# Sums of weight quarters in a feed-forward layer: from VectorE to accumulating transfers

## The chip, the cores and the metric

The kernel runs on one core of one Trainium2 chip, as one launch. The metric is the device time of that launch in microseconds (us); the kernel before takes 2193.0 us (median of 3 runs, 2192.62 to 2193.12). The profile names the engines so: PE is the matmul engine (TensorE) and PEld its weight loads, DVE is VectorE, ACT is ScalarE, POOL is GpSimd, SP the engine that issues the loads from memory. Every engine works through its own queue in order; semaphores tie the queues together. About 0.2% of the time (4.4 us) is what a measurement of this kernel tells from no change.

## The reference

One decoder block on 512 tokens of width 2048, in float32: RMS norm, one combined input projection, eight heads of dilated sliding-window attention and eight heads of sparse attention (compressed, selected and window branches mixed by gates), group norms, an output projection, and then the part that this case is about:

```python
hn2 = rmsnorm(h, norm2_g[l])
h = h + (jax.nn.silu(hn2 @ w_gate[l]) * (hn2 @ w_up[l])) @ w_down[l]
return rmsnorm(h, final_g)
```

`w_gate` and `w_up` are 2048 x 5632, `w_down` is 5632 x 2048.

## The kernel before, in words

**Three matmuls for one.** Each float32 operand is held as a high part (rounded to the matmul's format, `h`) and a low part (what is missing, `l`), and a product is three matmuls: high by high, high by low, low by high (L162 to 165 and L1002 to 1005).

**Weights.** Weights stream in on SP's queue. A unit is 128 x 1024 numbers, 512 KB; `load_to` (L102) puts it into one of four rotating buffers `raw` (`LA = 4`). A load may start when the buffer's last readers are done. Each unit is used as two *halves* of 512 columns; a half is a `Job` (L121). `Job.first` runs the job's `load` and `prep`, then rounds the half to `wh` on ACT (L134). `Job.second` makes `wl` on DVE (L137) and then runs the job's `post`. `wh` and `wl` have five rotating buffers each.

**The order of work.** The program is one order written out by hand. PE takes halves one after the other through `next_half` (L170): on its way it issues the `first` of the job three places ahead and the `second` of the one two places ahead, and runs what has been put off with `later(n, ...)`, that is, n halves after the present one. So within the queues of ACT and DVE the splits of coming weights stand between the evacuations of finished products.

**The feed-forward stage.** The 5632 columns of gate and up are worked in 44 blocks of 128 (`FB`, index f). In a block the weights form four quarters: gate0 (upper 1024 rows of the gate columns, called A11), up0 (A21), up1 (A22) and gate1 (A12), and the activations four quarters B11, B12, B21, B22 (row half by token half; 256 tokens each). Instead of eight products of quarters there are seven, P1 to P7, in the manner of Strassen and Winograd, each of 2 halves x 4 weight blocks x 3 matmuls of 256 columns:

| product | weights | activations |
|---|---|---|
| P1 | gate0 | B11 |
| P2 | gate1 | B21 |
| P3 | gate1 - (up0 + up1 - gate0) | B22 |
| P4 | up1 | T4 |
| P5 | up0 + up1 | T1 |
| P6 | up0 + up1 - gate0 | T2 |
| P7 | gate0 - up0 | T3 |

T1 to T4 are sums of activation quarters, made once by `terms` (L915). The sums of weight quarters are made anew in every block, in place in the `raw` buffers, by `comb` (L750) in `quad_jobs` (L743): four 128 x 512 operations on DVE per half column, eight per block. `ORDER0` is the order of the products in block 0, `ORDER` that in the others.

`product` (L990) issues the matmuls; P2 adds into P1's accumulator bank, and in blocks after the first P3 adds into P5's. `after` (L1020) reads the banks on ACT and DVE and puts gate and up together; `finish` (L1007) makes silu(gate) x up and splits it into high and low for the down product.

**Down products.** Every four blocks (`PH = 4`) the 16 row blocks of the down product for the last four column blocks are worked in (`down`, L1053). They stand between the products of blocks 4, 8, ..., 40: a *down job* is one load of 256 KB (`rawd`, two buffers), one split, and 12 matmuls of 512 columns. Blocks without them are called plain here: of blocks 1 to 43 these are 33, in 11 runs of three. The last down product comes after block 43 (`last`, L1091), with its weights (`fin`) in the `raw` buffers.

Of the kernel before, what the change touches and what calls it, by code (L numbers as in the profile page):

```python
# [71 lines left out]
def block_kernel(ctx: ExitStack, tc: tile.TileContext, xt, wst, wdn, smalls, wg, w2c, bias, ident_in, out):  # L72
# [24 lines left out]

    raws = {}
    state = {"dma": 0, "split": 0}
    LA = 4  # L100

    def load_to(n):  # L102
        while state["dma"] < min(n, len(units)):
# [66 lines left out]
    def next_half():  # L170
        i = pos["half"]
        pos["half"] += 1
        split_to(i + (AHEAD[i] if i < len(AHEAD) else 3 if i < len(jobs) - KB - 1 else 4))
        if i < n_plain:
            load_to(i // 2 + LA)
        while lag and lag[0][0] <= i:
            lag.popleft()[1]()
        j = jobs[i]
        return j.h, j.l
# [563 lines left out]
    def quad_jobs(f, order):  # L743

        u = base_u + 4 * f

        def q(i, k):
            return raws[u + i][:, 512 * k:512 * k + 512]

        def comb(o, a, b, op):  # L750
            return lambda: dve.tensor_tensor(o(), a(), b(), op=op)  # L751

        def nxt(i):
            return lambda: load_to(u + 4 + i + 1)

        r = {}
        for k in range(2):
            A11, A21, A22, A12 = (lambda i=i, k=k: q(i, k) for i in range(4))
            if f == 0:
                def s1(A11=A11, A21=A21, A22=A22):  # L760
                    comb(A11, A11, A21, OP.subtract)()
                    comb(A21, A21, A22, OP.add)()

                r["P1", k] = Job(A11, load=nxt(-1))
                r["P5", k] = Job(A21, prep=s1)
                r["P7", k] = Job(A11)
                r["P4", k] = Job(A22)
            else:
                r["P1", k] = Job(A11)
                r["P7", k] = Job(A11, prep=comb(A11, A11, A21, OP.subtract))  # L770
                r["P4", k] = Job(A22, post=comb(A21, A21, A22, OP.add))
                r["P5", k] = Job(A21)
            r["P6", k] = Job(A22, prep=comb(A22, A22, A11, OP.subtract))
            r["P2", k] = Job(A12)
            r["P3", k] = Job(A12, prep=comb(A12, A12, A22, OP.subtract))
        if f + 1 < FB:
            if f == 0:
                r["P6", 1].post = nxt(1)
                r["P3", 1].post = nxt(3)
            else:  # L780
                r["P6", 1].post = nxt(0)
                r["P5", 1].post = nxt(1)
                r["P3", 1].post = nxt(3)
        else:
            r["P6", 1].post = lambda: load_fin(1)
            r["P5", 1].post = lambda: load_fin(2)
            r["P3", 1].post = lambda: load_fin(LA)
        r["P1", 0].even = f in (1, 2) or f % 8 == 5
        return [r[p, k] for p in order for k in range(2)]

    ORDER0 = ("P1", "P5", "P2", "P7", "P4", "P6", "P3")
    ORDER = ("P1", "P7", "P4", "P6", "P5", "P2", "P3")

    def dn_job(p, nb):
        return Job(lambda: dn[p, nb], post=load_dn)
# [119 lines left out]
    def terms(nb):  # L915

        h, k, n = hs[:, nb, :], hs[:, nb % 8, :], nb % 8
        g, gk = gain2(nb), gain2(nb % 8)
        sq = ps.tile([128, S], F32, tag="sc", name="sq", bufs=2)
        t = ps.tile([128, S], F32, tag="t", name="tm", bufs=2)  # L920

        def stt(o, a, b, op):
            dve.scalar_tensor_tensor(o, a, b, t[:, LO] if op != OP.bypass else t[:, HI], op0=OP.mult, op1=op)

        def sums():
            if nb:
                dve.tensor_tensor(sacc, sacc, sq, op=OP.add)

        def squares():
            act.activation(sq if nb else sacc, h, AF.Square)  # L930

        if nb < 8:
            def s1():
                dve.tensor_tensor(t[:, LO], h[:, HI], h[:, LO], op=OP.subtract)
                squares()
                high("B11", n, h[:, LO], g)
                high("T1", n, t[:, LO], g)

# [12 lines left out]
        def s2():  # L951
            dve.scalar_tensor_tensor(t[:, LO], h[:, HI], g, t[:, LO], op0=OP.mult, op1=OP.subtract)
            sums()
            low("B21", n, h[:, LO], g)
            high("T3", n, t[:, LO])

        def s3():
            dve.scalar_tensor_tensor(t[:, HI], k[:, LO], gk, t[:, LO], op0=OP.mult, op1=OP.add)
            low("T3", n, t[:, LO])
            high("T2", n, t[:, HI])  # L960

        def s4():
# [24 lines left out]

    st = {}

    def product(f, name):  # L990
        key = {"P2": "P1", "P3": "P5" if f else "P3"}.get(name, name)
        if key == name:
            st[key] = banks[name]
        p = st[key][:, :256]
# [12 lines left out]
    def finish(f, g, u, c):  # L1007
# [3 lines left out]

        def up():
            dve.tensor_tensor(u, u, g, op=OP.mult)
            act.activation(h, u, AF.Copy)

        n = 0 if c == LO else 1
        later(n, up)
        later(n + 1, lambda: dve.tensor_tensor(l, u, h.bitcast(F32), op=OP.subtract))

    def after(f, name):  # L1020

# [3 lines left out]
        def add(o, a, b):  # L1025
            dve.tensor_tensor(o, a, b, op=OP.add)

        g, u = st.get("g"), st.get("u")
        if name == "P1":
            st["g"] = ft()  # L1030
            st["u"] = ft() if f else None
            act.activation(st["g"][:, LO], x("P1"), AF.Copy)
        elif name == "P6":
            add(g[:, HI], g[:, LO], x("P6"))
            add(u[:, LO], g[:, HI], x("P7"))
            if not f:
                dve.tensor_tensor(g[:, LO], x("P1"), st["r2"][:, LO], op=OP.mult)
                add(u[:, HI], u[:, LO], x("P5"))
                add(u[:, LO], u[:, LO], x("P4"))
                add(g[:, HI], g[:, HI], x("P5"))  # L1040
        elif name == "P5":
            add(u[:, HI], u[:, LO], x("P5"))
            add(u[:, LO], u[:, LO], x("P4"))
        elif name == "P2":
            dve.tensor_tensor(g[:, LO], x("P1"), st["r2"][:, LO], op=OP.mult)
            if f == FB - 1:
                finish(f, g, u, LO)
        elif name == "P3":
            add(g[:, HI], g[:, HI], x("P5" if f else "P3"))
            dve.tensor_tensor(g[:, HI], g[:, HI], st["r2"][:, HI], op=OP.mult)  # L1050
            finish(f, g, u, HI if f == FB - 1 else slice(0, 512))

# [18 lines left out]
    for kind, a, b in sched:  # L1071
# [5 lines left out]
        if f == 0:  # L1077
# [7 lines left out]
                st["u"] = ft()  # L1085
            if name in ("P1", "P6", "P3"):
                later(0 if name == "P1" else 1, lambda name=name: after(0, name))
        elif name in ("P1", "P6", "P5", "P2", "P3"):
# [145 lines left out]
```

## Time and profile before

| what | value |
|---|---|
| median of 3 runs | 2193.0 us |
| profiled execution | 2195.16 us |
| its span, first to last instruction | 2193.4 us |
| granted PE clock, mean | 0.996 |
| mean DMA rate, share of the 16 DMA engines taken by loads and stores | 105 GB/s, 33.2% |
| bytes read from and written to memory | 223.94 MB, 4.19 MB |
| loads of 512 KB into `raw` | 311 |
| loads of 256 KB into `rawd` | 160 |
| DVE sums in `raw` (L751) | 352, 241.7 us busy |

How to read the views: a group of instructions has its line, engine, operation, out<-in tiles with their shape and count, then busy time, mean ns of one, and the idle time of the engine just before them with what ended it. A wait has the waiting instruction, the one that released it, and total us, times, longest us. A row of a stage gives busy time and count of PE, PEld, DVE, ACT and POOL, then the granted PE clock (1.00 is full), the busy share of the DMA engines and their GB/s. Matmuls overlap each other: 0.28 us is the time of one of 256 columns from start to end, not the distance to the next. "To landing" is the time from the issue of a transfer to its completion.

### The profile page before, as it was taken

Reading aid. Unit: us, or ns where it says so; the run is one execution under the profiler, and the core shown is the slowest. Engines: PE = TensorE matmul, PEld = TensorE weight load, DVE = VectorE, ACT = ScalarE, POOL = GpSimd, SP = SyncE. Lnnn points to the kernel's source line nnn. Section 1 sums busy time; section 2 is a strip of 40 time slices with the busy share of each in tenths; the row PEclk is TensorE's granted clock in tenths of the full one; section 3 lists DMA queues with packets and bytes.
Section 4 is the critical chain, followed back from the end, with each engine's and each line's share of the span. In section 5 each row is a group of like instructions: output and inputs, shape, how many; then the busy total and the mean of one; then the engine's idle time right before and its main releaser. Section 6 shows DMA issues by size and latency. Waiting matters only on the chain.

```text
span 2193.4 us, 35893 instructions
## 1 busy us (share of the span) xinstructions
PE 2170.9 (99%) x13856; PEld 1950.1 (89%) x13856; DVE 1572.6 (72%) x3051; ACT 969.4 (44%) x1861; POOL 39.4 (2%) x46
## 2 busy tenths in 40 slices
PE   9999999999999999999999999999999999999997
PEld 7788888888887888989899999989898999999897
DVE  6755656356667578979687786869596877778686
ACT  6444444344444255535344443435253434434356
POOL 0000000000000000000000000000000000000003
PEclk9999999999999999999999999999999999999998
DMA  6432222322224332332333233333433333333243
GB/s 222 143 131 86 80 80 68 100 88 80 67 90 154 99 99 72 116 107 96 110 110 108 88 120 102 107 96 116 115 97 105 108 111 92 116 106 102 86 122 106
DMA packets 82252, 230.47 MB, mean 105 GB/s; under 512 B 8736, under 2 KB 13216, under 8 KB 82080
## 3 DMA queue, kind: packets, MB, share of 16 engines
q1 hardware_dynamic: 82080, 228.17, 33.2%
q8 instruction: 109, 1.79, 0.3%
q14 instruction: 63, 0.52, 0.1%
HBM read 223.94 MB, written 4.19 MB: 104 GB/s over the span
## 4 chain that ended last, share of the span: by engine, by line
PE 96%; DVE 3%; ACT 1%; DMA 0%; issue 0%; SPq 0%; DVEq 0%; ACTq 0%
PE P L1005 13%; PE P L1003 12%; PE P L1004 12%; PE pp L163 6%; PE pp L165 6%; PE pp L164 6%; PE pd L165 4%; PE pd L164 4%; PE pd L163 4%; PE P L165 3%; PE P L164 3%; PE P L163 3%; PE pab L164 3%; PE pab L165 3%; PE pab L163 3%; PE pt L512 1%
## 5 line engine op out<-in xcount | busy, mean ns | idle before, releaser
L134 ACT ACTIVATE wh<-raw 128x512 fp32r<-128x512 f32 x888 | 548.2, 628 | 520.4 <-PE P L1004 172.0
L137 DVE TENSOR_TENSOR wl<-raw,wh 128x512 fp32r<-128x512 f32 x888 | 597.5, 687 | 65.1 <-ACT wh L134 64.6
L1005 PE MATMUL P<-ah,wl 128*128 128x256 f32 x1056 | 292.0, 277 | 0.4 <-DVE wl L137 0.4
L1003 PE MATMUL P<-ah,wh 128*128 128x256 f32 x1056 | 291.9, 276 | 0.0
L1004 PE MATMUL P<-al,wh 128*128 128x256 f32 x1056 | 291.7, 276 | 0.0
L163 PE MATMUL pp<-ah,wh 128*128 128x512 f32 x640 | 260.7, 407 | 0.0
L165 PE MATMUL pp<-ah,wl 128*128 128x512 f32 x640 | 250.8, 392 | 0.0
L164 PE MATMUL pp<-al,wh 128*128 128x512 f32 x640 | 250.5, 391 | 0.0
L751 DVE TENSOR_TENSOR raw<-raw 128x512 f32<-128x512 f32 x352 | 241.7, 687 | 3.5
L134 ACT ACTIVATE wh<-rawd 128x512 fp32r<-128x512 f32 x160 | 101.0, 631 | 280.9 <-PE pd L164 164.8
L1003 PEld LDWEIGHTS P<-ah,wh 128*128 128x128 f32 x1056 | 198.4, 188 | 0.8
L1005 PEld LDWEIGHTS P<-ah,wl 128*128 128x128 f32 x1056 | 198.4, 188 | 0.9 <-DVE wl L137 0.8
L1004 PEld LDWEIGHTS P<-al,wh 128*128 128x128 f32 x1056 | 198.4, 188 | 0.9
L1067 DVE TENSOR_TENSOR hs<-hs,pd 128x512 f32<-128x512 f32 x98 | 67.4, 688 | 131.8 <-PE pd L165 131.7
L165 PE MATMUL pd<-ah,wl 128*128 128x512 f32 x392 | 154.4, 394 | 0.0
L164 PE MATMUL pd<-al,wh 128*128 128x512 f32 x392 | 153.7, 392 | 0.0
L163 PE MATMUL pd<-ah,wh 128*128 128x512 f32 x392 | 152.1, 388 | 0.0
L165 PEld LDWEIGHTS pp<-ah,wl 128*128 128x128 f32 x640 | 120.3, 188 | 28.0
L163 PEld LDWEIGHTS pp<-ah,wh 128*128 128x128 f32 x640 | 120.7, 189 | 19.7
L164 PEld LDWEIGHTS pp<-al,wh 128*128 128x128 f32 x640 | 120.8, 189 | 19.4
L137 DVE TENSOR_TENSOR wl<-rawd,wh 128x512 fp32r<-128x512 f32 x160 | 109.8, 686 | 23.9 <-ACT wh L134 23.2
L501 ACT ACTIVATE e<-e,st 128x512 f32<-128x512 f32 (+1 forms) x96 | 54.1, 564 | 135.4 <-DVE st L499 135.4
(277 smaller groups left out, 4922.8 us busy)
## 6 DMA issues: line engine op xcount, KB each, us to landing
raw<-in_wst_dram SPq DMA_DIRECT2D x311, 512.0 KB, 3.5
rawd<-in_wdn_dram SPq DMA_DIRECT2D x160, 256.0 KB, 2.6
bias<-in_bias_dram SPq DMA_DIRECT2D x16, 320.0 KB, 2.9
xc<-in_xt_dram SPq DMA_DIRECT2D x16, 256.0 KB, 2.7
hs<-in_xt_dram SPq DMA_DIRECT2D x16, 256.0 KB, 5.2
fin<-in_wdn_dram SPq DMA_DIRECT2D x8, 512.0 KB, 3.8
out_dram<-hs SPq DMA_DIRECT2D x10, 256.0 KB, 2.2
out_dram<-hs SPq DMA_DIRECT2D x3, 512.0 KB, 3.4
```

The lines of the kernel that those rows point to most:

```text
L134: act.activation(self.h, self.src(), AF.Copy)
L137: dve.tensor_tensor(self.l, self.src(), self.h.bitcast(F32), op=OP.subtract)
L163: pe.matmul(o, wh, mh, start=start, stop=False)
L164: pe.matmul(o, wh, ml, start=False, stop=False)
L165: pe.matmul(o, wl, mh, start=False, stop=stop)
L501: act.activation(et, et, AF.Exp, bias=m, scale=-1.0, accum_out=den)
L512: pe.transpose(p[:, 128 * (o + b):128 * (o + b) + 128], self.e[t][:, 128 * b:128 * b + 128], ident)
L751: return lambda: dve.tensor_tensor(o(), a(), b(), op=op)
L1003: pe.matmul(o, wh, mh, start=start, stop=False, skip_group_check=True)
L1004: pe.matmul(o, wh, ml, start=False, stop=False, skip_group_check=True)
L1005: pe.matmul(o, wl, mh, start=False, stop=stop, skip_group_check=True)
L1067: dve.tensor_tensor(hs[:, nb, :], hs[:, nb, :], p, op=OP.add)
```

## The change

In blocks 1 to 43 the sums are no longer made on DVE. A `post` of a job issues, on POOL's queue, a transfer from one `raw` buffer to another that adds to what is there (`plus`). There are four per half column, 256 KB each: after P1's split gate0 becomes gate0 + up0; after P4's, up0 becomes up0 + up1; after P7's, up1 becomes up1 + (gate0 + up0); after P6's, up1 becomes gate1 + all of that, and P3 takes it from there. A transfer only adds, so the products are those of the same scheme with the up columns negated: up comes out with the opposite sign, T1 changes its sign in `terms`, and `finish` turns the sign when it splits the result (a scale of -1 on ACT, a fused operation on DVE in place of a subtraction). Block 0 keeps its sums on DVE, in the new form (`here`).

The order of the products in blocks 1 to 43 becomes P1, P4, P7, P5, P6, P2, P3: each transfer stands four halves ahead of the split that reads its result. `raw` gets a fifth buffer, while the look-ahead of loads outside the blocks stays at four units; the next block's loads are issued after P4's second half (gate0), P6's first (up0) and second half (up1), and P3's second half (gate1). P3 adds into P5's bank only in the blocks with down jobs; in the others it has a bank of its own (`own`), and DVE makes one more add. What was read from the banks after P6 and after P5 is now read in one go after P6.

```diff
-    LA = 4
+    LA = 5
...
         if i < n_plain:
-            load_to(i // 2 + LA)
+            load_to(i // 2 + 4)
...
-        def comb(o, a, b, op):
-            return lambda: dve.tensor_tensor(o(), a(), b(), op=op)
-
-        def nxt(i):
-            return lambda: load_to(u + 4 + i + 1)
+        def plus(o, x):
+
+            return lambda: pool_e.dma_start(o(), x(), accum_op=OP.add)
+
+        def here(o, x):
+            return lambda: dve.tensor_tensor(o(), o(), x(), op=OP.add)
+
+        def load(i):
+            if f + 1 < FB:
+                return lambda: load_to(u + 4 + i + 1)
+            return lambda: load_fin((1, 2, 3, LA)[i])
...
             A11, A21, A22, A12 = (lambda i=i, k=k: q(i, k) for i in range(4))
-            if f == 0:
-                def s1(A11=A11, A21=A21, A22=A22):
-                    comb(A11, A11, A21, OP.subtract)()
-                    comb(A21, A21, A22, OP.add)()
-
-                r["P1", k] = Job(A11, load=nxt(-1))
-                r["P5", k] = Job(A21, prep=s1)
-                r["P7", k] = Job(A11)
-                r["P4", k] = Job(A22)
+            r["P1", k] = Job(A11)
+            r["P4", k] = Job(A22)
+            r["P7", k] = Job(A11)
+            r["P5", k] = Job(A21)
+            r["P6", k] = Job(A22)
+            r["P2", k] = Job(A12)
+            r["P3", k] = Job(A22)
+            if f:
+                r["P1", k].post = plus(A11, A21)
+                r["P4", k].post = plus(A21, A22)
+                r["P7", k].post = plus(A22, A11)
+                r["P6", k].post = plus(A22, A12)
             else:
-                r["P1", k] = Job(A11)
-                r["P7", k] = Job(A11, prep=comb(A11, A11, A21, OP.subtract))
-                r["P4", k] = Job(A22, post=comb(A21, A21, A22, OP.add))
-                r["P5", k] = Job(A21)
-            r["P6", k] = Job(A22, prep=comb(A22, A22, A11, OP.subtract))
-            r["P2", k] = Job(A12)
-            r["P3", k] = Job(A12, prep=comb(A12, A12, A22, OP.subtract))
-        if f + 1 < FB:
-            if f == 0:
-                r["P6", 1].post = nxt(1)
-                r["P3", 1].post = nxt(3)
-            else:
-                r["P6", 1].post = nxt(0)
-                r["P5", 1].post = nxt(1)
-                r["P3", 1].post = nxt(3)
-        else:
-            r["P6", 1].post = lambda: load_fin(1)
-            r["P5", 1].post = lambda: load_fin(2)
-            r["P3", 1].post = lambda: load_fin(LA)
+                if not k:
+                    r["P1", k].load = load(-1)
+                r["P5", k].prep = both(here(A11, A21), here(A21, A22))
+                r["P6", k].prep = here(A22, A11)
+                r["P3", k].prep = here(A22, A12)
+        for name, k, i in (("P4", 1, 0), ("P6", f == 0, 1), ("P6", 1, 2), ("P3", 1, 3)):
+            j = r[name, k]
+            j.post = both(j.post, load(i)) if j.post else load(i)
...
-    ORDER = ("P1", "P7", "P4", "P6", "P5", "P2", "P3")
+    ORDER = ("P1", "P4", "P7", "P5", "P6", "P2", "P3")
...
-                dve.tensor_tensor(t[:, LO], h[:, HI], h[:, LO], op=OP.subtract)
+                dve.tensor_tensor(t[:, LO], h[:, LO], h[:, HI], op=OP.subtract)
...
+    def own(f):
+
+        return f == 0 or f % PH > 0
+
     def product(f, name):
-        key = {"P2": "P1", "P3": "P5" if f else "P3"}.get(name, name)
+        key = {"P2": "P1", "P3": "P3" if own(f) else "P5"}.get(name, name)
...
-            act.activation(h, u, AF.Copy)
+            act.activation(h, u, AF.Copy, scale=-1.0)
...
-        later(n + 1, lambda: dve.tensor_tensor(l, u, h.bitcast(F32), op=OP.subtract))
+        later(n + 1, lambda: dve.scalar_tensor_tensor(l, u, -1.0, h.bitcast(F32), op0=OP.mult, op1=OP.subtract))
...
         elif name == "P6":
-            add(g[:, HI], g[:, LO], x("P6"))
+            sub(g[:, HI], g[:, LO], x("P6"))
             add(u[:, LO], g[:, HI], x("P7"))
+            add(u[:, HI], u[:, LO], x("P5"))
+            sub(u[:, LO], u[:, LO], x("P4"))
+            if own(f):
+                add(g[:, HI], g[:, HI], x("P5"))
             if not f:
                 dve.tensor_tensor(g[:, LO], x("P1"), st["r2"][:, LO], op=OP.mult)
-                add(u[:, HI], u[:, LO], x("P5"))
-                add(u[:, LO], u[:, LO], x("P4"))
-                add(g[:, HI], g[:, HI], x("P5"))
-        elif name == "P5":
-            add(u[:, HI], u[:, LO], x("P5"))
-            add(u[:, LO], u[:, LO], x("P4"))
...
         elif name == "P3":
-            add(g[:, HI], g[:, HI], x("P5" if f else "P3"))
+            add(g[:, HI], g[:, HI], x("P3" if own(f) else "P5"))
```

More of the change, by code (lines that the diff above doesn't have):

```diff
@@ L748, in q, with both, go @@
             return raws[u + i][:, 512 * k:512 * k + 512]
-        def comb(o, a, b, op):
-            return lambda: dve.tensor_tensor(o(), a(), b(), op=op)
-        def nxt(i):
-            return lambda: load_to(u + 4 + i + 1)
+        def plus(o, x):
[6 more added lines that the diff above has]
+            return lambda: load_fin((1, 2, 3, LA)[i])
+        def both(*fs):
+            def go():
+                for g in fs:
+                    g()
+            return go
         r = {}
@@ L1087, in block_kernel @@
                 later(0 if name == "P1" else 1, lambda name=name: after(0, name))
-        elif name in ("P1", "P6", "P5", "P2", "P3"):
+        elif name in ("P1", "P6", "P2", "P3"):
             later({(FB - 1, "P2"): 0, (FB - 1, "P3"): 3}.get((f, name), 1), lambda f=f, name=name: after(f, name))
```

2 lines of the change are left out of this document (added).

## The prediction

> **What bounds the kernel now.** I read the busy table first, then the stages, the waits and the order of time inside the feed-forward stage. The first view is the page's table of busy time.
>
> ```profile
> span 2193.4 us, 35893 instructions
> PE 2170.9 (99%) x13856; PEld 1950.1 (89%) x13856; DVE 1572.6 (72%) x3051; ACT 969.4 (44%) x1861; POOL 39.4 (2%) x46
> ```
>
> TensorE is occupied for 99% of the span, but a busy matmul engine need not be at its pace. So the second view splits the span into stages; columns are PE, PEld, DVE, ACT and POOL busy time, granted clock, DMA share and GB/s. The fifth line is one plain block (no down products inside); the last covers two blocks, with 16 down jobs between the products of the second.
>
> ```profile
> 0.00:890.00 890.00, 879.39 (x4441) 738.20 (x4442) 568.09 (x1326) 408.22 (x901) 19.79 (x22) 1.00 0.32 104
> ...
> 1050.00:1400.00 350.00, 350.00 (x2503) 326.34 (x2502) 266.32 (x453) 145.59 (x245) 0.00 (x0) 1.00 0.34 104
> 1400.00:1800.00 400.00, 400.00 (x2870) 373.38 (x2869) 304.13 (x517) 166.62 (x279) 0.00 (x0) 1.00 0.37 107
> ...
> 2150.00:2193.00 43.00, 31.56 (x263) 30.82 (x261) 24.44 (x54) 23.09 (x52) 12.67 (x17) 0.87 0.29 99
> ...
> 1001.39:1020.43 19.04, 19.04 (x171) 19.04 (x169) 17.69 (x32) 9.99 (x18) 0.00 (x0) 1.00 0.34 110
> 1039.47:1121.49 82.02, 82.02 (x530) 74.13 (x529) 56.39 (x95) 30.12 (x51) 0.00 (x0) 1.00 0.34 103
> ```
>
> The matmul engine is idle for 10.6 us before the feed-forward stage and 11.4 us at the very end, and not at all between. The third view is the order of time inside the plain block: the fourth high-by-high matmul of three products that follow each other, and of the first one's successor a block later.
>
> ```profile
> 1001.39 0.28 PE L1003 MATMUL P<-T4h,wh 128*128 128x256 f32 x1
> ...
> 1004.11 0.28 PE L1003 MATMUL P<-ah,wh 128*128 128x256 f32 x1
> ...
> 1006.83 0.28 PE L1003 MATMUL P<-T1h,wh 128*128 128x256 f32 x1
> ...
> 1020.43 0.28 PE L1003 MATMUL P<-T4h,wh 128*128 128x256 f32 x1
> ```
>
> Each product takes 2.72 us, so 1.36 us per half (one job of 12 matmuls), without a gap: seven products, 19.04 us a block. The longer stretch holds two blocks and 16 down jobs: 82.02 - 2 x 19.04 = 43.94 us, 2.74 us for each down job. DVE works 17.69 of 19.04 us and is nearly full, yet the matmuls do not wait for it. The views of waits say so: nothing is listed for PE from 890 to 2150 us; over the whole span its largest items on this path are these, and ACT's waits show why.
>
> ```profile
> PE prb L240 <- DVE r L234: 3.9, 3, 1.8
> ...
> PE P L1005 <- DVE wl L137: 0.4, 2, 0.2
> ...
> ACT wh L134 <- PE pd L164: 205.0, 97, 2.2
> ACT wh L134 <- PE P L1004: 181.1, 267, 0.9
> ```
>
> ACT waits for PE to release `wh`: the weight splits run as far ahead as the five `wh` buffers let them. The stage is bound by matmuls alone, so taking work off DVE can return at most the 0.4 us. What the change can do here is harm: it can make the splits late.
>
> **The change part by part.** Durations of the operations involved, from the groups by line (busy us, mean ns), and the times from issue to landing of the 256 KB and the 512 KB loads:
>
> ```profile
> L134 ACT ACTIVATE wh<-raw 128x512 fp32r<-128x512 f32 x888 | 548.2, 628 | 520.4 <-PE P L1004 172.0 <-DVE raw L751 73.8 <-PE pab L164 53.1
> ...
> L137 DVE TENSOR_TENSOR wl<-raw,wh 128x512 fp32r<-128x512 f32 x888 | 597.5, 687 | 65.1 <-ACT wh L134 64.6
> ...
> L751 DVE TENSOR_TENSOR raw<-raw 128x512 f32<-128x512 f32 x352 | 241.7, 687 | 3.5
> ...
> L1026 DVE TENSOR_TENSOR ft<-ft,P 128x256 f32<-128x256 f32 x221 | 92.7, 420 | 10.4
> ...
> L252 DVE SCALAR_TENSOR_TENSOR al<-xc,sm,ah 128x512 fp32r<-128x512 f32 x16 | 12.0, 751 | 7.3 <-ACT ah L251 7.3
> ...
> L646 POOL TENSOR_TENSOR acc<-acc,osq 128x512 f32<-128x512 f32 x14 | 19.1, 1362 | 586.4 <-ACT osq L645 586.4
> ...
> L733 SPq DMA_DIRECT2D rawd<-in_wdn_dram x160: 327/328/432, 642.8 to 2058.6; - x160
> ...
> DMA to landing us min/median/max: 2.4/2.6/3.9
> ...
> L108 SPq DMA_DIRECT2D raw<-in_wst_dram x313: 327/328/807, 1.7 to 2109.3; - x157
> ...
> DMA to landing us min/median/max: 3.3/3.5/8.3
> ```
>
> *DVE's sums.* Blocks 1 to 43 lose 8 sums each: 344 x 0.687 = 236 us of DVE busy time. It lies beside the matmuls, so it returns nothing. Added on DVE: one 256-wide add in the 33 blocks where P3 keeps its own bank (33 x 0.42 = 14 us), and the fused form at the end of a block (751 against 687 ns, 45 times, 3 us). DVE's 17.69 us a plain block fall by about 5; these additions cost nothing beside that cover. The sign changes elsewhere keep the operation. Cost 0.
>
> *The transfers.* 344 transfers of 256 KB, issued on POOL's queue, each reading two places and writing one. Call L the time from the moment a transfer may start to its landing. Within a block and one half k, four of them are in series: gate0 += up0 (after P1's split), up0 += up1 (after P4's), up1 += gate0 (after P7's), up1 += gate1 (after P6's). The second overwrites what the first reads, the third what the second reads, so POOL holds each until the one before it has landed; behind a held one, POOL's queue holds the transfers of the other half too. ACT's split of P6 waits for the third, that of P3 for the fourth; behind these ACT holds the evacuations and the next block's splits, and PE waits for those.
>
> How long is the loop from P1's split to the next block's P1 split, if transfers set it? Three landings, 3 L; P6's split, 0.63 + 0.69; the fourth, L; the other half comes one DVE operation behind, 0.69; ACT splits P3's second half and the next P1, 0.63 + 0.63; DVE first has the five 256-wide adds that now come in one burst after P6, 5 x 0.42 = 2.10, then P1's low part, 0.69. Together 4 L + 6.06 us, against 19.04 us of matmuls.
>
> The splits enter a run of three plain blocks with a lead. Five `wh` buffers mean that a split may start four jobs before its product; at the end of a block with down products these are two down jobs and two P3 halves, 2 x 2.74 + 2 x 1.36 = 8.2 us, of which the split uses 1.32: 6.9 us to spare. A run of three is free as long as 3 x (4 L + 6.06) <= 57.12 + 6.9, that is L <= 3.82 us. Beyond it each us of L costs 12 us a run, and with 33 plain blocks there are 11 runs: 132 us. In a block with down products there is time enough (12 more jobs lie between the steps of the chain), and the lead is won back.
>
> *What is L?* No row of this trace shows an accumulating transfer, nor one issued by POOL. From below: 2.4 us, the fastest 256 KB load (as if the second read cost nothing); that gives no loss, and a gain is excluded since PE waits for nothing there. From above: 8.3 us, the slowest landing of 512 KB, a loss of 4.48 x 132 = 591 us. The nearest row is the median 512 KB load, 3.5 us, because two reads of 256 KB pass the engines. I add 0.33 us, one SP issue, for a descriptor list that POOL's program must write (POOL takes 1362 ns for an add that DVE does in 687), and 0.27 us because the DMA engines, 0.34 busy in a plain block, will be at least 0.68 busy and a transfer meets a load twice as often. L = 4.1 us: 0.28 x 132 = 37 us lost. This is a narrow place: 0.3 us less and nothing happens.
>
> The Trainium skill, "DMA: Bandwidth & Descriptors", section "Anatomy of one DMA", puts a transfer issued by GpSimd at about 2.0 us plus its bytes over 436 GB/s; that would be an estimated 2.6 us for 256 KB, or 3.2 us with both reads counted, and the sum would be 0. No run so far shows a GpSimd transfer; for the 512 KB loads, which SP issues, the trace has 3.5 us.
>
> *Loads and the fifth buffer.* The loads of the next block move: gate0's to P4, up0's and up1's to P6, gate1's stays at P3. Up0's load takes gate0's buffer and waits, on SP, for the third transfer of the second half: 3 x 4.1 + 0.69 = 13.0 us into the block, landed at 16.5, and the next block's first transfer wants it at 19 or later. Behind it on SP stand up1's load, wanted a product later, and in the next down block the down loads. 2.5 us of cover: cost 0; were it gone, each us late would delay the first transfer by as much. Outside the blocks the look-ahead stays four units, and PE's waits there name Spread's products, not loads: 0, with 2 us of gain as the bound.
>
> *Block 0* keeps its sums on DVE at the same points; the three loads move together. Cost 0, with the 0.4 us of PE waits as bound.
>
> *Sum.* The profiled execution took 2195.16 us, 1.8 outside its span and 2.2 above the median of 2193.0. 2195.2 + 37 = 2232; by the median, 2230 us.
>
> **The rivals.**
>
> *The transfers land in time* (L up to 3.82 us): no change, 2193 us, since neither DVE's relief nor the fifth buffer meets a wait of PE. This is the other side, and it decides at one number. For it: the 256 KB loads land in 2.6 us and the 512 KB ones in 3.5 us while sharing the engines. Against: both are issued by SP and read once. It also holds if the landings are not in series as I say (POOL lets the second start before the first has landed): then each split waits for one landing only, against four jobs and the lead. The skill's page above speaks for this rival.
>
> *The DMA engines fill up.* One plain block's loads, 2.1 MB, take 0.34 x 19.04 = 6.5 us of all engines. The transfers write as much: at one pass 6.5 us more, at two reads 13.0, together 19.5 us, more than the block's 19.04. Then every landing queues behind others; with L = 4.8 us the loss is 0.98 x 132 = 129 us, 2322 us. For it: the row's 110 GB/s at a share of 0.34. Against: that price is for reads from HBM, and the sums stay on chip.
> The Trainium skill, "Collectives: The Full Stack", section "The bandwidth ceiling", says that an add in the DMA path costs two source reads and so runs at half a copy's rate; no run so far shows it, and by it the share would be an estimated 1.02.
>
> *Faster.* DVE loses 5 of 17.7 us a plain block, and PE might be held by it in ways too short to be listed. PE's starts lie 0.113 us apart through the block, so this can be no more than 1 to 2 us.
>
> **How the numbers follow.** About 0.2%, 4.4 us, is what a measurement of this kernel can tell from no change. Forecast (L between 3.85 and 4.6): 0.46. In time: 0.33, nearly all within 0.2%. Engines full or L above 4.6: 0.17. Faster: 0.04. Faster by over 0.2% 0.04, within 0.33, slower 0.63. The range takes in no change and goes up to L = 4.7, 0.88 x 132 = 116 us: 2190 to 2310; about 0.15 is left above and little below. The likeliest case alone is 2197 to 2296.
>
> **What would show it.** DVE's sums in `raw` fall to 8; a POOL queue appears with 90 MB. If I am right, ACT's splits of P6 and P3 wait for `raw` transfers, PE waits for `wh` in the second and third plain block of a run and hardly in blocks with down products, and the median landing of a transfer is near 4 us. If the median is below 3.5 us and PE shows no waits from 890 to 2150 us, the first rival holds. If the DMA share in a plain block is above 0.9 and the loads' own landings grow well over 3.5 us, it is the second. I am wrong in the mechanism if PE's idle time is ended by a load, or if granted clock falls.

## The result, and the profile after

The changed kernel takes 2373.6 us (median of 4 runs, 2370.3 to 2379.8) against 2193.1 us before (median of 4 runs; one of them, at 4551.9 us, is left out of the ratio): a ratio of 1.083, 95% interval 1.080 to 1.086. It is 180 us slower. The direction was forecast, the size was not: 2230 us was predicted, and the result lies above the range.

The page of the changed kernel, its busy table, the groups of the transfers and of the weight splits, the software queue and the issues of section 6:

```profile
span 2372.5 us, 36545 instructions
PE 2257.2 (95%) x13856; PEld 2009.8 (85%) x13856; DVE 1385.3 (58%) x2740; ACT 953.1 (40%) x1861; POOL 339.8 (14%) x390
...
q0 software_dynamic: 49536, 90.20, 22.8%
...
L134 ACT ACTIVATE wh<-raw 128x512 fp32r<-128x512 f32 x888 | 533.5, 625 | 719.7 <-DMA raw<-raw 356.2
L752 POOL DMA_DIRECT2D raw<-raw x344 | 298.9, 893 | 1322.6 <-DVE wl L137 886.3
...
raw<-in_wst_dram SPq DMA_DIRECT2D x311, 512.0 KB, 4.1
raw<-raw POOLq DMA_DIRECT2D x344, 256.0 KB, 4.0
```

DVE is relieved, by 187 us (1572.6 to 1385.3; the prediction's figures, 236 less 17, would give 219), and all 344 transfers are there, 90 MB on their own queue. The idle time of ACT's splits of `raw`, which was ended mostly by PE before (`wh` buffers), is now ended for half by the transfers: 356 of 720 us. A transfer lands 4.0 us after its issue; the 512 KB loads went from 3.5 to 4.1 us.

The view of waits, largest items of this path for PE, ACT and POOL (us in total, times, longest):

```profile
ACT wh L134 <- DMA raw<-raw: 356.2, 159, 6.7
POOL raw L752 <- DMA raw<-raw: 195.1, 109, 4.0
...
PE P L1012 <- DVE ft L1055: 56.8, 31, 2.3
PE P L1012 <- ACT wh L134: 21.1, 33, 1.6
PE P L1014 <- DVE wl L137: 10.3, 46, 0.4
```

PE, which waited for nothing between 890 and 2150 us, now waits for a bank to be emptied (L1055), and for `wh` and `wl`. The stretch from 1400 to 1800 us, whose row of before stands in the prediction, answers with:

```profile
1400.00:1800.00 400.00, 373.40 (x2508) 343.25 (x2507) 214.49 (x367) 141.69 (x245) 83.42 (x96) 0.97 0.68 156
```

PE is idle for 26.6 of 400 us where it was never idle, the DMA share is 0.68 in place of 0.37, and the granted clock 0.97 in place of 1.00. (The stretch doesn't hold the same blocks in both kernels, so the numbers of matmuls aren't compared.)

The order of time on POOL in one plain block, from the first sums (one for each half column) to the next block's (start, busy, and in brackets the idle time ahead and what ended it):

```profile
1054.42 1.75 POOL L752 DMA_DIRECT2D raw<-raw  x2 [9.13 <-DVE wl L137]
1058.08 0.86 POOL L752 DMA_DIRECT2D raw<-raw  x1 [1.91 <-DMA raw<-raw]
1059.61 0.86 POOL L752 DMA_DIRECT2D raw<-raw  x1 [0.67 <-DMA raw<-raw]
1062.00 0.89 POOL L752 DMA_DIRECT2D raw<-raw  x1 [1.53 <-DMA raw<-raw]
1063.55 0.87 POOL L752 DMA_DIRECT2D raw<-raw  x1 [0.66 <-DVE al L1027]
1067.95 0.86 POOL L752 DMA_DIRECT2D raw<-raw  x1 [3.53 <-DMA raw<-raw]
1069.72 0.86 POOL L752 DMA_DIRECT2D raw<-raw  x1 [0.91 <-DVE wl L137]
1079.28 1.75 POOL L752 DMA_DIRECT2D raw<-raw  x2 [8.71 <-DVE wl L137]
```

This is the series of the prediction: first sum at 1054.42, second at 1058.08, third at 1062.00, fourth at 1067.95 (P6's split stands between), the next block at 1079.28. The loop is 24.9 us, against 19.04 us of matmuls. Its end on ACT, DVE and PE:

```profile
1073.56 0.63 ACT L134 ACTIVATE wh<-raw 128x512 fp32r<-128x512 f32 x1 [3.88 <-DMA raw<-raw]
1074.22 0.69 DVE L137 TENSOR_TENSOR wl<-raw,wh 128x512 fp32r<-128x512 f32 x1 [3.66 <-ACT wh L134]
...
1075.47 0.69 DVE L137 TENSOR_TENSOR wl<-raw,wh 128x512 fp32r<-128x512 f32 x1 [0.56 <-ACT wh L134]
...
1078.11 1.29 DVE L137 TENSOR_TENSOR wl<-raw,wh 128x512 fp32r<-128x512 f32 x2
...
1079.31 0.42 DVE L1055 TENSOR_TENSOR ft<-P,r 128x256 f32<-128x256 f32 x1
...
1079.88 0.36 PE L1012 MATMUL P<-B11h,wh 128*128 128x256 f32 x1 [2.05 <-DVE ft L1055]
```

PE waits 2.05 us, by the list for DVE's evacuation at L1055, an operation of 0.42 us. But that one stands on DVE's in-order queue behind P3's two low parts, the burst of five adds and P1's low parts, and P3's split began only when the fourth transfer landed. The name in the list of waits is the last link; the cause is a landing six microseconds earlier.

Where the time goes, block by block: the span on PE from one block's first product to the next one's, means by the block's place in its cycle of four (the first carries the down products), in us.

| kernel | with down products | 1st plain | 2nd plain | 3rd plain |
|---|---|---|---|---|
| before | 63.0 | 19.17 | 19.05 | 19.04 |
| after | 64.1 | 21.81 | 25.03 | 25.46 |

A run of three plain blocks grows by 2.64 + 5.98 + 6.42 = 15.04 us. Eleven of them, and ten blocks with down products at 1.1 us, make 176 of the 180 us.

### The profile page after: what moved, and what is told of

It reads as the page before. It is cut to its first block, busy times and chain, and to the rows that moved or that the text cites. A ratio compares the mean times of both kernels' runs of the same rounds, so it can differ in the third digit from the quotient of the medians.

```text
span 2372.5 us, 36545 instructions
## 1 busy us (share of the span) xinstructions
PE 2257.2 (95%) x13856; PEld 2009.8 (85%) x13856; DVE 1385.3 (58%) x2740; ACT 953.1 (40%) x1861; POOL 339.8 (14%) x390
## 5 line engine op out<-in xcount | busy, mean ns | idle before, releaser
L134 ACT ACTIVATE wh<-raw 128x512 fp32r<-128x512 f32 x888 | 533.5, 625 | 719.7 <-DMA raw<-raw 356.2
L752 POOL DMA_DIRECT2D raw<-raw x344 | 298.9, 893 | 1322.6 <-DVE wl L137 886.3
L1012 PE MATMUL P<-ah,wh 128*128 128x256 f32 x1056 | 299.4, 283 | 21.0 <-ACT wh L134 20.8
L1014 PE MATMUL P<-ah,wl 128*128 128x256 f32 x1056 | 301.8, 286 | 9.8 <-DVE wl L137 9.2
L1012 PE MATMUL P<-B11h,wh 128*128 128x256 f32 x352 | 110.8, 315 | 58.4 <-DVE ft L1055 56.8
```

Source lines behind the costliest of these rows:

```text
L134: act.activation(self.h, self.src(), AF.Copy)
L752: return lambda: pool_e.dma_start(o(), x(), accum_op=OP.add)
L1012: pe.matmul(o, wh, mh, start=start, stop=False, skip_group_check=True)
L1014: pe.matmul(o, wl, mh, start=False, stop=stop, skip_group_check=True)
```

## The experiments

The first run undoes the transfers alone: same order, signs, buffers and load places, but DVE adds.

```diff
-            return lambda: pool_e.dma_start(o(), x(), accum_op=OP.add)
+            return lambda: dve.tensor_tensor(o(), o(), x(), op=OP.add)
```

> Everything of the change stays (order of products, fifth buffer, own banks, the five adds in one burst, the signs), but each transfer is replaced by the same add on DVE at the same place. Series theory (the four landings in series per half column make the loop from one block's P1 split to the next 25 us): the loss is gone, 2190 to 2200 us. Traffic theory (the DMA engines or POOL are too full): the same. Order theory (the new order puts P1's bank evacuation behind the splits on DVE, and PE waits for it): most of the 180 us stays, above 2300 us.

Measured: 2228.8 us, ratio 1.016 (1.015 to 1.018), between what the theories gave. So 145 of the 180 us come with the transfers, and 36 us with the rest of the change. PE's list of waits from 890 to 2170 us holds 1.9 us in all, so these 36 us are not waits; their cause has a run of its own further on.

The second run cuts the series: each transfer adds a tile of zeros, so that the first three no longer need each other's result. (The sums themselves are left out.)

```diff
-            return lambda: pool_e.dma_start(o(), x(), accum_op=OP.add)
+            return lambda: pool_e.dma_start(o(), rest["zero"], accum_op=OP.add)
```

> Every transfer adds a constant tile of zeros instead of a quarter, so the sums are left out; count, bytes, targets and places stay. The second transfer no longer waits for the first, nor the third for the second; third to P6's split to fourth to P3's split stays. Series theory: the loop falls below 19 us, 2193 to 2225 us. Traffic theory: the same bytes and issues cost the same, above 2330 us. Order theory: above 2330 us.

Measured: 2305.0 us, ratio 1.051 (1.049 to 1.053), again between the theories. In the second and third plain blocks of a run the first, second and third are now issued 1.2 and 1.1 us apart (4.1 and 4.0 to 4.2 before), but they bunch: a landing takes 5.3 us (section 6), P6's split comes 7.4 us after the third is issued, and the fourth is still a landing in series. The loop falls there from 25.0 and 25.5 us to 22.7 and 22.9, not to 19.

```profile
ACT wh L134 <- DMA raw<-zero: 256.0, 144, 7.0
...
raw<-zero POOLq DMA_DIRECT2D x344, 256.0 KB, 5.3
```

The third run keeps every wait and every instruction, but each transfer moves 32 of its 512 columns:

```diff
+            return lambda: pool_e.dma_start(o()[:, :32], x()[:, :32], accum_op=OP.add)
```

> Each transfer adds 32 of its 512 columns, so most of each sum is left out; all waits stay. Issue to first packet was 1.43 us in the changed kernel and a 2 KB packet took 0.187 us, eight per engine, 1.5 us; with 128 B packets a landing should take 1.8 to 2.2 us. Series theory: 4 x 2.0 + 9.0 = 17 us, under 19.04: 2193 to 2200 us. Traffic theory by bytes: the same. If POOL's issue time (0.89 us each, unchanged) or the order were the cause: above 2330 us.

Measured: 2203.9 us, ratio 1.005 (1.003 to 1.006), 4 us above the range. With landings of 2.3 us (median), about 1 us under the shortest of the full size, almost nothing of the loss is left. POOL issues as many transfers as before, so its time for issuing them is not what costs. Half the columns, 256, in the same edit:

> Each transfer adds 256 of its 512 columns, so half of each sum is left out; packets become 1 KB. A landing should take 1.43 us + 8 x 0.1 + what contention leaves, about 3.0 us (2.3 us at 32 columns, 4.0 at 512). Series theory: 4 x 3.0 + 8.5 = 20.5 us, 1.5 us a plain block less the lead: 2205 to 2240 us. If the loss went with the bytes: half of it, about 2285 us.

Measured: 2267.8 us, ratio 1.034 (1.031 to 1.037), landing 3.0 us; between the series theory and the 2285 us by bytes. In the second and third plain blocks the first three steps did shrink (3.1 to 3.4, 3.4 and 2.8 us), but from the fourth sum to P3's split it still took 5.2 and 5.5 us.

Is it the waiting in series, or the mere traffic? The fourth run leaves the sums on DVE and adds transfers that nobody reads, from each split's `wl` to two scratch tiles.

```diff
+                dve.tensor_tensor(o(), o(), x(), op=OP.add)
+                n = rest["n"] = rest.get("n", 0) + 1
+                pool_e.dma_start(rest["ghost"][n % NG], r[name, k].l.bitcast(F32), accum_op=OP.add)
```

> The sums are made on DVE as in e1; beside them 344 transfers of the same size add each new low weight part to one of two scratch tiles that nobody reads, issued at the same places. Series theory: nothing of the weights waits for a transfer, 2193 to 2215 us. Traffic theory: the DMA engines are as full as in the changed kernel, loads come late, above 2300 us.

Measured: 2302.5 us, ratio 1.050 (1.047 to 1.052). It doesn't answer the question: the transfers held the `wl` buffers that they read, and DVE waited for them, so they were in the path after all (waits of DVE):

```profile
DVE wl L138 <- DMA ghost<-wl: 74.0, 47, 3.8
```

The fifth run mends that. The transfers read a constant, and a one-column add on POOL keeps each at the time when its sum would have been issued.

```diff
+                w = r[name, k].l.bitcast(F32)[:, :1]
+                pool_e.tensor_tensor(rest["pace"][:, n % 8:n % 8 + 1], w, w, op=OP.add)
+                pool_e.dma_start(rest["ghost"][n % 2], slot["B21h"][:, 32:544].bitcast(F32), accum_op=OP.add)
```

> As e4, but the unread transfers add a constant tile to the two scratch tiles, so that they hold no weight buffer; a one-column add on POOL in front of each lets it start when the low weight part is written, as in the changed kernel. The sums are made on DVE. What remains beside e1 (2229 us) is the traffic alone. Traffic theory: well above e1, 2290 us or more, because loads land late. Series theory: within 15 us of e1.

Measured: 2237.6 us, ratio 1.020 (1.017 to 1.023). The same bytes, with a landing of 4.5 us and loads at 4.4 us, cost 9 us over the first run, if nothing stands behind them.

```profile
raw<-in_wst_dram SPq DMA_DIRECT2D x311, 512.0 KB, 4.4
...
ghost<-B21h POOLq DMA_DIRECT2D x344, 256.0 KB, 4.5
```

One of its plain blocks, from one first product to the next, and the plain block of the changed kernel shown above:

```profile
1017.82:1037.68 19.86, 19.86 (x170) 19.86 (x169) 18.47 (x33) 9.81 (x17) 11.05 (x16) 1.00 0.94 215
```

```profile
1054.42:1079.28 24.86, 22.08 (x168) 21.50 (x168) 13.50 (x25) 10.13 (x18) 6.96 (x8) 0.93 0.81 177
```

In the first PE is never idle at a DMA share of 0.94; in the changed kernel it is idle for 2.8 us at a share of 0.81. So the engines have the throughput. What costs is that splits stand behind landings.

How many landings in series are free? The sixth run gives the fourth sum back to DVE, the seventh the third as well.

```diff
-                r["P6", k].post = plus(A22, A12)
+                r["P3", k].prep = here(A22, A12)
```

> The fourth sum (gate1) goes back to DVE, as a step before P3's split; three transfers per half column stay. The loop loses a landing (4.3 us) and the lag of the second half behind the first (2.9 us), and gains two DVE adds (1.2 us): 19 to 20 us. Series theory: 2195 to 2220 us. Traffic theory, by bytes: three quarters of the loss, about 2325 us.

Measured: 2277.0 us, ratio 1.038 (1.035 to 1.041), far above what was expected and half way to the rival's 2325 us. In one plain block (first sums at 1019.13 us) P6's split starts behind the three landings 11.25 us after the loop began, the second half column comes 2.7 us later, and another 8.2 us of in-order work on ACT and DVE stand behind it, which the expectation had not counted: a loop of 22.2 us. (The mean of the second and third plain blocks is 23.1 us.)

```diff
-                r["P7", k].post = plus(A22, A11)
-                r["P6", k].post = plus(A22, A12)
+                r["P6", k].prep = here(A22, A11)
+                r["P3", k].prep = here(A22, A12)
```

> The changed kernel with the first two sums as transfers and the third and the fourth on VectorE again, as preparation of P6 and P3. Theory (a series of landings and of the in-order work behind them): with three landings the loop was 3 x 3.75 + 2.7 + 8.2 = 22.2 us; with two it is about 2 x 3.7 + 2.7 + 9 = 19.1 us, just at the 19.04 us of TensorE in a plain block, so the waits all but go: 2225 to 2245 us, near the 2229 us of the kernel with all sums on VectorE, with plain blocks of 19.4 to 20.2 us. Rival (each transfer costs its own share by what it puts on the queues and engines, in proportion to their number): half way between none and four, (2229 + 2374) / 2 = 2300 us, 2285 to 2315.

Measured: 2216.2 us, ratio 1.011 (1.008 to 1.013), below the range of the first theory and far from the rival's. With two, the waits are gone; nothing on PE is over 0.5 us from 890 to 2170 us:

```profile
PE P L1014 <- DVE wl L137: 0.5, 2, 0.2
PE P L164 <- DVE al L1027: 0.3, 1, 0.3
PE P L1012 <- ACT wh L134: 0.3, 1, 0.3
```

The sum of PE's gaps of more than 150 ns at full clock in this stage is 4.3 us with DVE adds alone, 3.1 with two transfers, 49.0 with three and 111.4 with four: no share for each transfer, but a threshold between two and three.

The eighth run shortens the end of the loop: the burst of five adds after P6 is put off by two halves in plain blocks. (In the last block the adds then come after P1's and P2's evacuation, so its sums are not the reference's.)

```diff
-            later({(FB - 1, "P2"): 0, (FB - 1, "P3"): 3}.get((f, name), 1), lambda f=f, name=name: after(f, name))
+            later({(FB - 1, "P2"): 0, (FB - 1, "P3"): 3}.get((f, name), 3 if name == "P6" and f % PH else 1), lambda f=f, name=name: after(f, name))
```

> The changed kernel with one edit: in plain blocks the five adds after P6 are put off by two more halves, so on DVE they stand behind the low parts of the next P1 instead of ahead of them. They took 2.03 us of the loop. Series theory with the loop of 25 us: 23 us, 2.0 x 33 = 67 us less, 2300 to 2320 us. If PE's wait for P1's bank (57 us listed) is the bound by itself, nothing is won: 2360 us or more.

Measured: 2404.5 us, ratio 1.096 (1.093 to 1.100), in the wrong direction. From P3's second split to the next block's first sum it took 2.3 us in place of 4.4, as meant. But from the next block's first sum to its second it then took 5.8 us in place of 4.1, and from the fourth to P3's split 5.7 to 6.7 in place of 4.3 to 4.7: moved earlier, the transfers met the loads of the next block (the first sum lands after 5.4 us in place of 3.7, the median landing is 4.6 us), and the loop came to 26.1 and 26.3 us. What part the loads have was the next question; in this run they leave the plain blocks.

```diff
             if f + 1 < FB:
+                if f % PH:
+                    return lambda: raws.__setitem__(u + 4 + i, raws[u + i])
                 return lambda: load_to(u + 4 + i + 1)
```

> The changed kernel, in which the three plain blocks of each cycle issue no weight loads: the blocks after them use the buffers as they are, so their weights (and the sums in them, which go on growing over one cycle) are not the reference's. The loads of the block that carries a down projection stay, and so do all transfers, waits and products. Theory (four transfers in series, each lengthened by the 512 KB loads that are issued beside the fourth): in the changed kernel the loop was 4 x 4.0 + 9.0 us. Without loads the landing falls to near the shortest one seen, 3.2 us, the loop of a plain block to about 4 x 3.2 + 9.0 = 21.8 us, the 6.7 us of the first plain block's fourth transfer to under 4, and the time to 2225 to 2260 us. Rival (the transfers take 4 us by themselves, or delay each other, and the loads have no part in it): loops stay at 25 us and the time at 2340 to 2375 us. Rival (without the loads the series is hidden again): blocks of 19.6 us as with the sums on VectorE, 2225 us or less, with the gaps of over 150 ns on TensorE gone.

Measured: 2512.9 us, ratio 1.146 (1.143 to 1.149), outside all that was expected, by a fault of the edit: the loads left out were all made up in the block with down products. Section 6 shows 303 of 311:

```profile
raw<-in_wst_dram SPq DMA_DIRECT2D x303, 512.0 KB, 4.1
```

That block went from 64.1 to 78.5 us; ten times the difference is 144 us, and the run is 139 us slower than the changed kernel. The run tells nothing of the plain blocks alone. The next version leaves them out for good:

```diff
+    def skip(n):
+        while state["dma"] <= n:
+            raws[state["dma"]] = raws[state["dma"] - 4]
+            state["dma"] += 1
...
+                if f % PH:
+                    return lambda: skip(u + 4 + i)
```

> The changed kernel, in which the three plain blocks of each cycle issue no weight loads and none are made up for later (128 of the 311 loads of 512 KB are gone): the blocks after them use the buffers as they are, so their weights (and the sums in them, which go on growing over one cycle) are not the reference's. The loads that the block with the down projection issues stay, and so do all transfers, waits and products. Theory (four transfers in series, each lengthened by the loads that run beside them): the landing falls towards the shortest seen, 3.2 us, the loop of a plain block to about 4 x 3.2 + 9.0 = 21.8 us, the fourth transfer of the first plain block from 6.7 us to under 4, and the time to 2225 to 2280 us. Rival (the transfers take 4 us by themselves and by each other, and the loads have no part in it): loops stay at 25 us and the time at 2340 to 2375 us.

Measured: 2302.9 us, ratio 1.050 (1.048 to 1.052): between the two. Section 6 and the stretch from 1400 to 1800 us:

```profile
raw<-in_wst_dram SPq DMA_DIRECT2D x183, 512.0 KB, 3.7
raw<-raw POOLq DMA_DIRECT2D x344, 256.0 KB, 3.5
```

```profile
1400.00:1800.00 400.00, 385.88 (x2701) 357.00 (x2700) 230.31 (x394) 152.64 (x262) 85.53 (x99) 1.00 0.54 113
```

Without loads the fourth sum of the first plain block takes 3.8 us until P3's split, not 6.7; the others 3.6 and 3.7, not 4.3 and 4.7; the second half column comes 2.1 us behind, not 2.3 to 3.1. The steps to the second and third sum stay at 3.9 to 4.6. So leaving out the loads beside the transfers takes away 71 of the 180 us. What stays is 74 us over the first run, or 109 us over the kernel before, and it is read as the cost of the series itself.

The last run is about the 36 us that came without a transfer. In the kernel before, the first half of P1 takes a place 64 bytes further on in its buffer in some blocks (`even`). Here it never does, and nothing else is changed:

```diff
-        r["P1", 0].even = f in (1, 2) or f % 8 == 5
+        r["P1", 0].even = False
```

> The kernel before, in which the first half column of P1 never takes the place 64 bytes further on, which it has in the blocks 1, 2 and every eighth block from 5. No instruction is added or taken away. If TensorE has two paces at full clock (113.3 and 117.8 ns for a matmul of 256 columns), into the second of which it falls at a small hiccup and from which that one half column brings it back, then stretches of blocks run at 117.8 ns with no waits in the profile, and the time is 2200 to 2250 us. If the place of the half column has no such effect, the time stays within 3 us of 2193 and every plain block of the second half takes 19.05 us.

Measured: 2224.9 us, ratio 1.015 (1.013 to 1.016). From 1030 to 1400 us PE is never idle, at a granted clock of 1.00, as in the kernel before. What differs is how far apart its matmuls start:

```profile
1030.00:1400.00 370.00, 370.00 (x2601) 346.33 (x2600) 278.21 (x470) 151.16 (x253) 0.00 (x0) 1.00 0.34 104
```

```profile
1068.13 0.28 PE L1003 MATMUL P<-T4h,wh 128*128 128x256 f32 x1
...
1070.49 0.28 PE L1005 MATMUL P<-T4h,wl 128*128 128x256 f32 x1
```

The two matmuls are 20 apart: 2.36 us / 20 = 118 ns, against 2.72 us / 24 = 113.3 ns before (the products in the prediction). Every plain block takes 19.8 us. Summed over the stage, starts that lie at the slower pace cost 31.4 us here and gaps nothing; in the first run, with DVE adds, the slower pace costs 27.7 of its 34 us of excess on PE. That the same pace carries those 36 us is read from the starts in both traces. What switches the pace is not settled. In the kernel before, every return to the faster pace comes at P1 of a block with the moved half column (blocks 1, 2, 5, 13, 21, 29 and 37). In the first run, which keeps these places, only those of blocks 1, 2, 21 and 29 brought it back, each time until the next block's P1, and two returns came elsewhere. In this run it stayed slow. So the place matters, but does not decide alone.

## Why the prediction was wrong

The form was right: four landings in series set a loop, the loop overruns the matmuls in a run of three plain blocks, the lead absorbs a part, and the blocks with down products win it back. The size was not. The loop of a plain block, term by term; measured values are means over the plain blocks, from the starts of POOL's transfers and ACT's splits.

| term of the loop | predicted us | measured us |
|---|---|---|
| first sum to second | 4.1 | 4.00 |
| second to third | 4.1 | 4.26 |
| third to P6's split | 4.1 | 3.61 |
| P6's split to the fourth | 1.32 | 1.73 |
| fourth to P3's split | 4.1 | 5.23 |
| lag of the second half column | 0.69 | 2.75 |
| P3's second split to the next first sum | 4.05 | 4.36 |
| loop | 22.46 | 25.94 |

- *L was right*: 4.0 us in the median against 4.1. That is in part luck: the shortest landing is 3.2 us, not the 3.5 + 0.33 of the prediction, and the median lies 0.7 above it, not 0.27. L was called the narrow place, and it wasn't where the error lay.
- *"The other half comes one DVE operation behind, 0.69"* failed: 2.75 us. This is the largest error, 2.06 x 33 = 68 us. A transfer consists of 128 packets of 2 KB and 16 of 4 bytes; the large ones took 187 ns in the median, so 8 on each of 16 engines are an estimated 1.5 us in which it fills them all. The second half column's transfer can therefore hardly follow at a lag of 0.69 us. The lag was costed on DVE, where it no longer was. No run changed it alone, but it is 1.2 us with 256 columns, 1.0 with 32, and 2.1 without loads in the plain blocks: most of it goes with what the transfers move, and some 0.6 us with the loads.
- *The fourth transfer as long as the others* failed: 5.23 us, and 6.7 in the first plain block, where it meets the two 512 KB loads that the change itself moved to P6. 1.13 x 33 = 37 us. The prediction put the moved loads at 0 because they come in time; what they do to a transfer beside them it counted only as 0.27 us in every L. Removing the loads brought the step to 3.7 us. And with 32 columns, in the second and third plain blocks, the fourth transfer of the first half column still landed after 4.4 and 4.6 us, those of the first three sums after 2.1 to 2.6.
- *The lead of 6.9 us* was too much. Measured from the start of P1's low part to its first matmul, it falls from 7.3 us at the beginning of a run to 1.8: 5.5 us to spend. 1.4 x 11 = 15 us. It is gone within the first plain block.
- *Blocks with down products free*: 1.1 us each, 11 us for ten. The first run has 1.3 us there without a transfer, so this is not taken for the series' doing.
- The two smaller terms of the table, 0.41 and 0.31, less the 0.43 that the first three steps came in under, make 0.29 x 33 = 10 us.

37 forecast + 68 + 37 + 15 + 11 + 10 = 178 us, against 180 measured.

The rule of the prediction, with 5.5 in place of 6.9, also holds for the experiments. Three loops less 57.1 us of matmuls less 5.5 us of lead, beside what three plain blocks took longer than before (57.3 us):

| kernel | three loops us | by the rule | measured |
|---|---|---|---|
| after | 77.9 | 15.3 | 15.0 |
| burst put off | 78.1 | 15.5 | 17.3 |
| no loads in plain blocks | 71.3 | 8.7 | 8.5 |
| constant source | 70.0 | 7.4 | 7.2 |
| 256 columns | 68.1 | 5.5 | 5.3 |
| 32 columns | 62.4 | -0.2 | 0.3 |

The loops in this table are measured in each run, so it tests only the last step, from the loop to PE's time, and not what makes a loop long. With 32 columns the first plain block's loop, 23.2 us, is held by PE itself: ACT's splits of P6 there wait for its matmuls.

- *The transfers land in time* is refuted by the waits and by the 145 us between the changed kernel and the first run. Its other form (not in series) is refuted by POOL's order of time.
- *The DMA engines fill up* gave 2322 us, nearer the result, but by another mechanism: the share in the plain block shown is 0.81, not above 0.9, L is 4.0, not 4.8, and unread transfers cost 9 us in all, with a share of 0.94 in a plain block. What was right in it is that transfers and loads lengthen each other, at single places and not on average.
- *DVE's relief returns nothing* held. The other edits at cost 0 did not hold together: the first run, with all of them, took 36 us more, most of it at the slower pace of the matmuls. In the changed kernel PE waits for the loop, so in plain blocks this pace is not taken to come on top: the rule above leaves nothing for it. So the 36 us cannot simply be added to the terms above.
- *Wrong if the granted clock falls*: it fell, to 0.97 from 1400 to 1800 us. Between 890 and 2320 us there were 18 stretches of 3.4 us and one of 6.8 at half the clock, in which matmuls lost about 30 us. The rule leaves no time over for them, so they are read as a result of the waits and not as their cause; no run took them away alone.
- *PE waits in the second and third plain block and hardly in those with down products*: right, except that the first plain block too grew, by 2.64 us. That the waits are mostly listed under L1055, a bank, and not under `wh` was not foreseen.

No version tried beats the kernel before. It leaves PE without a gap in this stage, so moving sums off DVE had nothing to win.

## What to carry to other kernels

Before a sum is moved from an engine at 0.7 us to a transfer, count how many landings come to stand in series between one use of a buffer and the next, and add everything that stands behind the last of them on in-order queues; here two were free and three were not, although DVE had been the busier engine and the DMA engines were not full. The two transfers of a pair issued 0.6 us apart landed 1.4 to 1.6 us apart, about the time that one of them fills the engines, and one issued beside a large load later still, so cost each at its place and not by its median. And when the waits list names a short operation, look at what stands before it on its queue: the wait for the bank began at a transfer.

## What the runs showed of the hardware

- An accumulating transfer of 256 KB within the chip's buffers lands 3.2 us after its issue at best and 4.0 in the median here. The first packet came 1.43 us after the issue at the earliest; a 2 KB packet took 187 ns, against 84 ns for a 2 KB packet of a load (medians). POOL's instruction took 0.86 us in the median and 0.89 in the mean.
- The matmuls of 256 columns have two paces at full granted clock, 113.3 and 118 ns. Moving one half column of weights by 64 bytes in some blocks was worth 33 us in the kernel before (2224.9 against 2192.3); in the changed order, with the same places, it did not keep the faster pace.
- In the changed kernel the granted clock halved for 3.4 us 18 times, and once for 6.8, between 890 and 2320 us, where the longest listed wait of a matmul is 2.3 us. In the kernel before it did not halve between 890 and 2150 us.
- 344 transfers that read one constant tile, the first three of a half column not held by each other, landed in 5.3 us (median), against 4.0 in the changed kernel. They were issued 1.1 to 1.2 us apart, so this is read as their delaying each other.
